# The first weights of an encoder trunk: a weight piece in two halves on two queues, a reordered load, and a store on another queue

## The chip, the cores and the metric

One core of a Trainium2 chip runs the whole program. The metric is the device time of one execution in microseconds (us); a comparison takes the median of several. In this program TensorE (PE) multiplies, VectorE (DVE), ScalarE (ACT) and GpSimd (POOL) work on its results, and SyncE (SP) starts most transfers. Each engine carries out its own instructions in order.

## The reference

Two sequences, a prompt of 2048 tokens and a sample of 512, with 1024 channels, pass through two layers and a final RMSNorm, all in float32:

```python
def attention_layer(x, g, w_in, w_out, sink, rel_bias):
    h = rmsnorm(x, g)
    z = h @ w_in
    q, k, v, gate = ...          # 1024, 256, 256 and 1024 columns; 16 heads, 4 kv heads
    o = banded_gqa_with_sink(q, k, v, rel_bias, sink)   # |i-j| <= 128
    return x + (o * jax.nn.silu(gate)) @ w_out

def fourier_layer(x, g, w_gate, w_out):
    h = rmsnorm(x, g)
    f = jnp.fft.fftn(hg, axes=(1, 3), norm="ortho").real   # 4 channel groups
    return x + (f * jax.nn.silu(h @ w_gate)) @ w_out
```

`rel_bias` gives each head a bias by the distance of query and key.

## The kernel before, in words

Every float32 product is made of three faster ones. An operand `a` is kept as a rounded part and a remainder (`hi`, `lo`), and `matmul3` (lines 90 to 94) issues hi by hi (L92), hi by lo (L93) and lo by hi (L94) into one PSUM bank. So each weight, once loaded in float32 (a tile `w32...`), is rounded by ACT (L113) and subtracted by DVE (L120) or POOL (L118) before PE can use it. `load_w` does this; a piece is 128 rows by 1024 columns, 512 KB. Pieces 8 and 9 of `w_in` hold the K weights, four blocks of 256 columns each: piece 8 has the blocks of k = 0 to 3 (k counts the eight blocks of 128 input channels), piece 9 those of k = 4 to 7. Pieces 10 and 11 hold the V weights in the same way. Pieces 0 to 7 are Q, 12 to 19 the gate.

The tokens go in chunks of 512. The sample is chunk 0 and comes first. For it `make_h(0, None)` loads the eight tiles `xk` of the transposed input (256 KB each, L180) and scales them by the norm's weight `g0s` into the two parts of `h` (ACT L186, DVE L187). The division by the root mean square comes later: `stats` loads the tokens a second time (`xs`, L149), squares and sums them on ACT (L150), and `inv_rms` makes the reciprocal root, ending in one POOL instruction (L87, `inv`). `spread` brings it into the layout of the products with four transposes on PE (L164).

At the very start PE runs 12 warm-up products on a zero tile (`idle`, L206). Then `kv_proj` makes K (`kp`, 48 products, k outermost), one small product `bp` for the bias rows (L222), and V (`vp`, 96 products of half the width, k outermost in four banks); its evictions are L317 and L318, K's L266 and L267. After that come Q and gate (`qp`, `gp`) of the first pair of heads, p = 0, and from then on attention for p in between Q and gate for p + 1.

`bias_rows` copies `bp` into the tile `brow` (DVE L224) and stores it in `rowd` in HBM (L225); each pair of heads reads its biases back from there (`b`, L381).

Which instruction stands where in an engine's order is decided when the program is built, by a scheduler with estimated costs; `after(...)` adds an order by hand. A transfer is started by an instruction in the order of one engine, its queue: SP for loads, POOL for the stores of the split weights (`wsd`, L122). A transfer's instruction that waits holds up all that stands behind it in that engine's order. The order on SP's queue at the start is: `g0s`, piece 8, eight `xk`, pieces 9 and 10, the one-hot table and the small tables for the bias, four `xs`, piece 11, the store of `rowd`, then Q and gate weights and the first `b`.

Of the kernel before, what the change touches and what calls it, by code (L numbers as in the profile page):

```python
# [9 lines left out]
F32R = mybir.dt.float32r  # L10
# [3 lines left out]
ALU = mybir.AluOpType  # L14
# [4 lines left out]
P = 128  # L19
D = 1024  # L20
# [11 lines left out]
LINE = 512  # L32
# [7 lines left out]
def f32(ap):  # L40
    return ap.bitcast(F32)
# [3 lines left out]
def encoder(  # L45
# [3 lines left out]
    PE, ACT, DVE, POOL, SP = nc.tensor, nc.scalar, nc.vector, nc.gpsimd, nc.sync  # L49
# [5 lines left out]
    wp = wstack.enter_context(tc.tile_pool(name="wp", bufs=1, side="right"))  # L55
# [5 lines left out]
    mhalf = cpool.tile([P, 8], F32, name="mhalf")  # L61
    POOL.memset(mhalf, -0.5)
    g0s = cpool.tile([P, KD], F32, name="g0s")
    SP.dma_start(g0s, g0.rearrange("(k p) -> p k", p=P))

    x1d = dram.tile([T, D], F32, name="x1d")
    s2d = [dram.tile([n, D], F32, name=f"s2d{i}") for i, n in enumerate((SEQ, DEC))]
# [7 lines left out]
    def bank(name):  # L75
        return psum.tile([P, 512], F32, tag="bank", name=name)

    def xtile(shape, dtype, name):
        return xp.tile(shape, dtype, align_bytes=LINE, tag="x", bufs=4, name=name)
# [16 lines left out]
    def load_w(c, n, name, lo_engine=None, late=None):  # L96

        w = wp.tile([P, 2, D], F32R, align_bytes=LINE, tag="w", bufs=4, name=f"w{name}")
        if c == 1 and n in AGAIN:
            w32 = xtile([P, D], F32, f"w32{name}")  # L100
            SP.dma_start(w32, w_in[n])
            ACT.copy(w[:, 0], w32)
            DVE.tensor_tensor(w[:, 1], w32, f32(w[:, 0]), ALU.subtract)
            POOL.dma_start(f32(wsd[n]), f32(w))
            return w[:, 0], w[:, 1]
        if c:
            SP.dma_start(f32(w), f32(wsd[n]))
            return w[:, 0], w[:, 1]
        w32 = stage[late is not None or n > 19 or n in (6, 7, 18, 19)](f"w32{name}")
        load = SP.dma_start(w32, w_in[n] if n < 20 else w_out[(n - 20) // 4, (n - 20) % 4])  # L110
        if late:
            after(load, late)
        ACT.copy(w[:, 0], w32)  # L113
        if lo_engine is None:

            for i in range(4):
                cs = slice(i * 256, i * 256 + 256)
                POOL.tensor_tensor(w[:, 1, cs], w32[:, cs], f32(w[:, 0, cs]), ALU.subtract)  # L118
        else:
            lo_engine.tensor_tensor(w[:, 1], w32, f32(w[:, 0]), ALU.subtract)  # L120
        if late or n not in LATE + AGAIN:
            (SP if lo_engine else POOL).dma_start(f32(wsd[n]), f32(w))  # L122
        return w[:, 0], w[:, 1]

    stage, res_tile, ready = [], [], {}

    def after(ins, anchor):

        if anchor is not None:
            tc.add_manual_dep(ins.ins, anchor.ins.name, ISSUE, reason="issue order")  # L130

    def attention_phase():

        with ExitStack() as es:
# [20 lines left out]
            def spread(c, inv, place=None):  # L155

                tok, lo_t, hi_t = CHUNKS[c]
                nt = min(640, hi_t - tok) // P
                invb = ap.tile([P, 640], F32, tag="invb", name=f"invb{c}")
                for i0 in range(0, nt, 4):  # L160
                    m = min(4, nt - i0)
                    ps = bank(f"ib{c}_{i0}") if place is None else place
                    for i in range(m):
                        PE.transpose(ps[:, i * P : (i + 1) * P], inv[:, i0 + i : i0 + i + 1].to_broadcast([P, P]), ident)  # L164
                    ACT.copy(invb[:, i0 * P : (i0 + m) * P], ps[:, : m * P])  # L165
                return invb

            def make_h(c, invb):

                tok, lo_t, hi_t = CHUNKS[c]  # L170
                n = min(640, hi_t - tok)
                hs, halo = [], []
                for k in range(KD):
                    if invb is None:
                        if k % 2 == 0:
                            xk2 = wp.tile([P, 2, CH], F32, align_bytes=LINE, tag="uT", bufs=8, name=f"xk{c}_{k}")
                        xk = xk2[:, k % 2]
                    else:
                        xk = xtile([P, D], F32, f"xk{c}_{k}")[:, :640]
                    SP.dma_start(xk[:, :n], xT[k * P : (k + 1) * P, tok : tok + n])  # L180
                    if invb is not None:
                        last_mul[0] = POOL.tensor_tensor(xk[:, :n], xk[:, :n], invb[:, :n], ALU.mult)
                        after(last_mul[0], last_evac[0])
                    h = main.tile([P, 2, CH], F32R, align_bytes=LINE, tag="hT", bufs=8, name=f"h{c}_{k}")
                    gk = g0s[:, k : k + 1]
                    hi = ACT.activation(h[:, 0, :], xk[:, :CH], AF.Copy, scale=gk)  # L186
                    lo = DVE.scalar_tensor_tensor(h[:, 1, :], xk[:, :CH], gk, f32(h[:, 0, :]), ALU.mult, ALU.subtract)  # L187
                    after(hi, last_u[0])
                    after(lo, last_u[1])
                    hs.append((h[:, 0], h[:, 1]))  # L190
                    if n > CH:
                        if k % 4 == 0:
                            hl = ap.tile([P, 4, 2, P], F32R, align_bytes=LINE, tag="qab", bufs=2, name=f"hl{c}_{k}")
                        ACT.activation(hl[:, k % 4, 0], xk[:, CH:], AF.Copy, scale=gk)
                        DVE.scalar_tensor_tensor(
                            hl[:, k % 4, 1], xk[:, CH:], gk, f32(hl[:, k % 4, 0]), ALU.mult, ALU.subtract
                        )
                        halo.append((hl[:, k % 4, 0], hl[:, k % 4, 1]))
                return hs, halo
# [6 lines left out]
                PE.matmul(ps, idle[:, :P], idle, start=True, stop=True)  # L206

            last_u = [None, None]
            early = [load_w(0, 8, "k0_0", DVE)]
            hs, halo = make_h(0, None)  # L210
            early.append(load_w(0, 9, "k0_1", DVE))

            def bias_rows():

                rowd = dram.tile([NH, 512], F32, name="rowd")
                rb = ap.tile([33, NH], F32, tag="tmp", bufs=2, name="rb")
                DVE.memset(rb[32:33], 1.0)
                SP.dma_start(rb[:32], rel_bias)
                oh = ap.tile([33, 512], F32, tag="s", bufs=2, name="oh")
                SP.dma_start(oh, onehot)  # L220
                bp = bank("bp")
                PE.matmul(bp[:NH], rb, oh, start=True, stop=True)  # L222
                brow = ap.tile([NH, 512], F32, tag="tmp", bufs=2, name="brow")
                DVE.tensor_copy(brow, bp[:NH])  # L224
                SP.dma_start(rowd, brow)  # L225
                sk = ap.tile([P, NH], F32, tag="sk", name="sk")
                SP.dma_start(sk, bass.AP(sink.tensor, sink.offset, [[0, P], [1, NH]]))
                DVE.tensor_scalar(sk, sk, -1.0, None, ALU.mult)
                return rowd, sk
# [390 lines left out]
            def first_norms():  # L620
                bias.extend(bias_rows())
                return [s() for s in stats(0)][-1]

            for c in range(len(CHUNKS)):

                if c > 1:
                    hs, halo = make_h(c, invb)
                for s in tail:
                    s()
                if c == 1:  # L630
                    hs, halo = make_h(c, invb)
# [4 lines left out]
                rowd, sk = bias  # L636
# [7 lines left out]
                for i in range(64 + LAG + AVLAG):  # L644
                    p, n = divmod(i, 8)
# [14 lines left out]
                    if c + 1 < len(CHUNKS):  # L660
# [4 lines left out]
                        elif i == 56:  # L665
                            invb = spread(c + 1, inv)
# [8 lines left out]
                    k = i - LAG  # L675
# [20 lines left out]
    def fourier_phase(tail):  # L696
        with ExitStack() as es:
# [522 lines left out]
            for i, f in enumerate(pend):  # L1220
                finish(*f, last=i == len(pend) - 1)

    fourier_phase(attention_phase())


# [96 lines left out]
```

## Time and profile before

| | us |
|---|---|
| three runs | 1663.11, 1664.0, 1667.96 |
| median | 1664.0 |
| the profiled execution | 1665.56 |
| its span, first to last instruction | 1663.8 |
| PE busy in it | 1640.0 |
| ACT busy in it | 873.8 |
| DVE busy in it | 1172.5 |

How to read the lines of a profile here: in the timeline, a row has its start and duration in us, the engine (PEld is PE's weight load, SPq the transfers that SP issues), the line of the kernel, the operation, the tile written and the tiles read with the shapes, how many instructions the row merges, and in brackets the idle time before it with what ended it. In the waits, a row names who waited for whom, with the total in us, the number of times and the longest.

### The profile page before, as it was taken

How to read it: one execution, taken by the hardware profiler on the slowest of the kernel's cores; microseconds unless marked ns; L12 is line 12 of the kernel's file. 1: busy time of each engine (PE TensorE's matmuls, PEld its weight loads, DVE VectorE, ACT ScalarE, POOL GpSimd, SP SyncE). 2: the span in 40 equal slices, each digit the busy share in tenths (PEclk: the TensorE clock that was granted, in tenths of full speed). 3: DMA queues.
4: the chain of work that ended last, by engine and by line, in shares of the span. 5: the costliest groups of instructions: out<-in, count | busy, mean ns of one | idle time of the engine just before them, and what ended most of it. 6: DMA issues, size and time to landing. Idle time of an engine off the chain costs nothing.

```text
span 1663.8 us, 25654 instructions
## 1 busy us (share of the span) xinstructions
PE 1640.0 (99%) x8987; PEld 1410.4 (85%) x8987; DVE 1172.5 (70%) x2810; ACT 873.8 (53%) x1998; POOL 382.3 (23%) x536
## 2 busy tenths in 40 slices
PE   9999999999999999999999999999999999999997
PEld 7888788888898888988888888888888887888886
DVE  5787665888548886478874688768676769888553
ACT  6788644676236674256752466555554545342321
POOL 2465642112402113121122211221111111101000
PEclk9999999999999999999999999999999999999999
DMA  7486886454864456754549644556556578553331
GB/s 276 162 303 232 286 329 227 160 194 156 289 227 164 159 190 221 249 206 155 189 146 329 231 158 158 225 197 230 184 199 234 184 247 319 165 190 125 113 127 51
DMA packets 90252, 340.49 MB, mean 205 GB/s; under 512 B 11099, under 2 KB 21339, under 8 KB 72716
## 3 DMA queue, kind: packets, MB, share of 16 engines
q1 hardware_dynamic: 71676, 261.50, 46.0%
q0 software_dynamic: 18160, 76.56, 11.8%
q8 instruction: 72, 1.18, 0.3%
q10 hardware_dynamic: 288, 0.79, 0.1%
q14 instruction: 56, 0.46, 0.1%
HBM read 263.28 MB, written 75.53 MB: 204 GB/s over the span
## 4 chain that ended last, share of the span: by engine, by line
PE 82%; DVE 5%; ACT 5%; DMA 4%; issue 2%; POOL 1%; SPq 0%; DVEq 0%; POOLq 0%; ACTq 0%
PE spt L404 5%; PE av L457 5%; PE pt L443 5%; PE qp L92 4%; PE qp L94 4%; PE qp L93 4%; PE gp L92 4%; PE gp L94 4%; PE gp L93 4%; PE op L92 4%; PE op L94 3%; PE op L93 3%; PE fo L93 3%; PE fo L94 3%; PE fo L92 3%
## 5 line engine op out<-in xcount | busy, mean ns | idle before, releaser
L420 ACT ACTIVATE S<-S 128x385 f32<-128x385 f32 (+1 forms) x320 | 191.0, 597 | 46.8 <-DVE S L416 45.3
L444 ACT CAST pts<-pt 128x384 fp32r<-128x384 f32 (+1 forms) x320 | 144.2, 453 | 109.1 <-PE pt L443 104.5
L445 DVE TENSOR_TENSOR pts<-pt,pts 128x384 fp32r<-128x384 f32 (+1 forms) x320 | 168.3, 527 | 43.9 <-ACT pts L444 40.7
L416 DVE CUSTOM_DVE_ANT_0 S<-spt,b 128x385 f32<-128x385 f32 (+1 forms) x320 | 168.8, 528 | 34.7 <-PE spt L404 31.6
L404 PE MATMUL spt<-kwin,qab 128*128 128x384 f32 (+1 forms) x640 | 157.2, 327 | 1.1 <-DVE S L416 1.1
L476 POOL TENSOR_TENSOR o<-o,s 128x256 f32<-128x256 f32 x75 | 55.4, 739 | 437.7 <-DVE o L474 437.4
L443 PE MATMUL pt<-ident,S 128*128 128x128 f32 x896 | 150.6, 273 | 0.7 <-ACT S L429 0.6
L404 PEld LDWEIGHTS spt<-kwin,qab 128*128 128x128 f32 x640 | 118.2, 188 | 26.9 <-DVE S L416 1.7
L457 PEld LDWEIGHTS av<-pts,v 128*128 128x128 f32 x896 | 126.4, 189 | 14.0 <-DVE qab L353 1.6
L92 PE MATMUL gp<-h,wg 128*128 128x512 f32 x320 | 137.8, 431 | 0.0
L92 PE MATMUL qp<-h,wq 128*128 128x512 f32 x320 | 136.9, 428 | 0.8 <-DVE v L318 0.8
L457 PE MATMUL av<-pts,v 128*128 128x256 f32 x896 | 136.1, 285 | 1.4 <-DVE qab L353 1.1
L92 PE MATMUL op<-wo,uT 128*128 128x512 f32 x320 | 126.5, 397 | 1.5 <-ACT invb L165 0.8
L92 PE MATMUL fo<-wo,tTu 128*128 128x512 f32 x320 | 125.8, 393 | 1.3 <-ACT wo L1124 1.3
L443 PEld LDWEIGHTS pt<-ident,S 128*128 128x128 f32 x896 | 113.6, 140 | 15.7 <-DVE pts L445 3.2
L94 PE MATMUL qp<-h,wq 128*128 128x512 f32 x320 | 126.1, 394 | 0.0
L94 PE MATMUL gp<-h,wg 128*128 128x512 f32 x320 | 125.9, 393 | 0.0
L93 PE MATMUL op<-wo,uT 128*128 128x512 f32 x320 | 125.8, 393 | 0.0
L93 PE MATMUL qp<-h,wq 128*128 128x512 f32 x320 | 125.8, 393 | 0.0
L93 PE MATMUL gp<-h,wg 128*128 128x512 f32 x320 | 125.7, 393 | 0.0
L93 PE MATMUL fo<-wo,tTu 128*128 128x512 f32 x320 | 125.4, 392 | 0.1
L94 PE MATMUL fo<-wo,tTu 128*128 128x512 f32 x320 | 124.7, 390 | 0.0
(356 smaller groups left out, 4089.6 us busy)
## 6 DMA issues: line engine op xcount, KB each, us to landing
wo<-wsd SPq DMA_DIRECT2D x32, 1024.0 KB, 5.0
wq<-wsd SPq DMA_DIRECT2D x31, 1024.0 KB, 4.9
wg<-wsd SPq DMA_DIRECT2D x31, 1024.0 KB, 6.4
x<-x1d SPq DMA_DIRECT2D x40, 512.0 KB, 3.9
b<-b21d SPq DMA_DIRECT2D x40, 512.0 KB, 5.8
b<-rowd SPq DMA_DIRECT2D x40, 384.0 KB, 4.4
xs<-in_x_dram SPq DMA_DIRECT2D x23, 512.0 KB, 6.8
s2d<-gt POOLq DMA_DIRECT2D x40, 256.0 KB, 3.7
```

The lines of the kernel that those rows point to most:

```text
L92: PE.matmul(out, a[0], b[0], start=start, stop=False, skip_group_check=more)
L93: PE.matmul(out, a[0], b[1], start=False, stop=False, skip_group_check=more)
L94: PE.matmul(out, a[1], b[0], start=False, stop=stop, skip_group_check=more)
L404: PE.matmul(ps[:, 2 + k0 * P : 2 + k1 * P], q, kwin[g][:, part, b * P + k0 * P : b * P + k1 * P], start=part == 0, stop=part == 1,)
L416: DVE.tensor_tensor_reduce(out=s[:, e0:e1], in0=ps[:, 1 + e0 : 1 + e1], in1=st["bias"][:, j, 386 - e1 : 386 - e0][:, ::-1], scale=1.0, sca ...
L420: last_exp[0] = ACT.activation(s[:, e0:e1], s[:, e0:e1], AF.Exp, bias=mn, scale=-1.0, accum_out=den)
L443: PE.transpose(ps[:, kb, :], s[:, 1 + kb * P : 1 + (kb + 1) * P], ident)
L444: ACT.copy(hi[:, k0:k1, j, :], ps[:, k0:k1, :])
L445: DVE.tensor_tensor(lo[:, k0:k1, j, :], ps[:, k0:k1, :], f32(hi[:, k0:k1, j, :]), ALU.subtract)
L457: PE.matmul(out, v, pt[:, kb].rearrange("p h q -> p (h q)"), start=kb == k0 and part == 0, stop=kb == k1 - 1 and part == 1,)
L476: eng.tensor_tensor(o, o, s, ALU.mult)
```

## The change

The first K weight piece (piece 8) is loaded as two halves of 512 columns, one by SP's queue and one by ACT's, and each half is rounded and subtracted by itself; the second half's two instructions stand behind `h` of k = 0. `g0s` is loaded by ACT's queue instead of SP's. Piece 9 is loaded, rounded and subtracted after `h` of k = 3 instead of after k = 7. The rows of the bias are stored by POOL's queue instead of SP's.

In the built program, on ACT the two transfers stand ahead of its table load. On PE, K's products at k = 1 and k = 4 change places among themselves, and in V at k = 4 the four rounded products and the four transposes of `spread` come before the first product that takes the remainder of piece 11. On ACT and DVE the rounding and subtracting of the first gate weights moves behind `spread`'s copy, and K's first evictions move a few places ahead. From the second pair of heads on, the instruction orders are the same.

```diff
     g0s = cpool.tile([P, KD], F32, name="g0s")
-    SP.dma_start(g0s, g0.rearrange("(k p) -> p k", p=P))
+    ACT.dma_start(g0s, g0.rearrange("(k p) -> p k", p=P))
...
-            def make_h(c, invb):
+            def make_h(c, invb, between={}):
...
                     hs.append((h[:, 0], h[:, 1]))
+                    if k in between:
+                        between[k]()
...
             last_u = [None, None]
-            early = [load_w(0, 8, "k0_0", DVE)]
-            hs, halo = make_h(0, None)
-            early.append(load_w(0, 9, "k0_1", DVE))
+
+            wk = wp.tile([P, 2, D], F32R, align_bytes=LINE, tag="w", bufs=4, name="wk0_0")
+            wk32 = stage[0]("w32k0_0")
+
+            def half(i):
+                cs = slice(i * 512, i * 512 + 512)
+                (SP, ACT)[i].dma_start(wk32[:, cs], w_in[8, :, cs])
+                return lambda: (
+                    tc.keep_in_program_order(ACT.copy(wk[:, 0, cs], wk32[:, cs])),
+                    DVE.tensor_tensor(wk[:, 1, cs], wk32[:, cs], f32(wk[:, 0, cs]), ALU.subtract),
+                )
+
+            halves = [half(i) for i in range(2)]
+            halves[0]()
+            early = [(wk[:, 0], wk[:, 1])]
+            hs, halo = make_h(0, None, {0: halves[1], 3: lambda: early.append(load_w(0, 9, "k0_1", DVE))})
...
                 DVE.tensor_copy(brow, bp[:NH])
-                SP.dma_start(rowd, brow)
+
+                POOL.dma_start(rowd, brow)
```

## The prediction

> **What bounds the kernel now.** I read the page's busy shares first, then PE's waits, then the timeline of the first 35 us, because every line of the change acts before that.
>
> ```profile
> PE 1640.0 (99%) x8987; PEld 1410.4 (85%) x8987; DVE 1172.5 (70%) x2810; ACT 873.8 (53%) x1998; POOL 382.3 (23%) x536
> PE kp L92 <- ACT h L186: 2.0, 1, 2.0
> PE qp L92 <- DVE v L318: 0.8, 1, 0.8
> SPq L225 <- DVE inv L86: 8.0, 1, 8.0
> ```
>
> PE is busy for 1640.0 of 1663.8 us, so 23.8 us of idle time is all that any reordering can win. The second line, from PE's waits, is the longest single one: 2.0 us before the first K product. The third is the gap before the first Q product. The last, from SP's queue, is the store of the bias rows, which holds SP for 8.0 us. All three lie where the change acts. The profiled execution took 1665.56 us (span 1663.8 and 1.76 around it), 1.56 above the median of 1664.0.
>
> The start, by the timeline:
>
> ```profile
> 1.18 4.07 PE L206 MATMUL idle<-idle 128*128 128x512 bf16 x12 [1.18 <-DVE idle L203]
> 0.73 0.44 SPq L64 DMA_DIRECT2D g0s<-in_g_dram  x1
> 1.23 0.57 SPq L110 DMA_DIRECT2D w32k<-in_w_in_dram  x1
> 5.58 1.04 ACT L113 CAST wk<-w32k 128x1024 fp32r<-128x1024 f32 x1 [3.57 <-DMA w32k<-in_w_in_dram]
> 6.53 5.01 ACT L186 ACTIVATE h<-xk,g0s 128x512 fp32r<-128x512 f32 x8
> 6.65 1.23 DVE L120 TENSOR_TENSOR wk<-w32k,wk 128x1024 fp32r<-128x1024 f32 x1 [4.29 <-ACT wk L113]
> 7.30 1.22 PE L92 MATMUL kp<-h,wk 128*128 128x512 f32 x2 [2.04 <-ACT h L186]
> 7.80 5.38 DVE L187 SCALAR_TENSOR_TENSOR h<-xk,g0s,h 128x512 fp32r<-128x512 f32 x8
> 8.60 0.79 PE L93 MATMUL kp<-h,wk 128*128 128x512 f32 x1
> 19.91 0.39 PE L94 MATMUL kp<-h,wk 128*128 128x512 f32 x1
> ```
>
> The warm-up ends at 5.25. The first weight piece (512 KB, issued at 1.23 behind g0s) lands at 5.58. ACT rounds it, then makes h of k=0; DVE takes the weight's low part (6.65 to 7.88) and only then h's (7.80 on), so the third K product starts at 8.60. The last of the 48 starts at 19.91; one step is 5.01/8 = 0.63 us on ACT and 5.38/8 = 0.67 on DVE.
>
> The granted clock and the transfers, from the windows (duration, PE, PEld, DVE, ACT, POOL, clock, DMA share, GB/s):
>
> ```profile
> 2.00:2.50 0.50, 0.50 (x3) 0.21 (x2) 0.33 (x2) 0.01 (x1) 0.00 (x0) 1.00 0.67 5
> 2.50:3.00 0.50, 0.50 (x3) 0.22 (x2) 0.00 (x0) 0.00 (x0) 0.00 (x0) 1.00 2.18 133
> 3.00:3.50 0.50, 0.50 (x3) 0.17 (x2) 0.00 (x0) 0.00 (x0) 0.00 (x0) 1.00 0.06 25
> 7.00:7.50 0.50, 0.20 (x1) 0.20 (x2) 0.50 (x1) 0.50 (x2) 0.00 (x0) 0.79 1.03 393
> 7.50:8.00 0.50, 0.50 (x2) 0.30 (x2) 0.50 (x2) 0.50 (x2) 0.00 (x0) 0.50 1.03 389
> 10.50:11.00 0.50, 0.50 (x3) 0.46 (x2) 0.50 (x2) 0.50 (x2) 0.00 (x0) 0.80 0.99 410
> 5.00:10.00 5.00, 2.88 (x7) 1.66 (x6) 3.35 (x5) 4.42 (x7) 0.00 (x0) 0.73 1.06 404
> ```
>
> A mean of 0.79 between 1.00 and 0.50 puts the fall at 7.29, one of 0.80 the recovery at 10.70: 3.41 us apart. In the 3.41 us before the fall (from 3.88) PE worked only 5.25 - 3.88 = 1.37 us, 40%. So the gap before the first K product costs twice: 2.0 us of waiting, then 3.4 us at half clock. Meanwhile the transfer engines are occupied but move almost nothing until 3.5 (5, 133, 25 GB/s): g0s's 1024 four-byte pieces go first. After that they run at 404 GB/s.
>
> **The change, part by part.** *First half of the weight piece.* It is the first transfer on SP, issued at 0.73 instead of 1.23, and half as big. The old one took 5.58 - 1.23 = 4.35 us, of which 1.30 is 512 KB at 404 GB/s; 3.05 is latency and g0s. Kept whole, that gives 0.73 + 3.05 + 0.65 = 4.43; with g0s's slow 1.0 us out of its way 3.4. I take 4.0. ACT now issues g0s and the second half itself, ahead of its table load: at the SP rows' 0.44 and 0.57 that ends near 1.75, hidden under the wait for data. The x tile of k=0 follows on SP while the second half shares the engines: 0.65 to 1.3 us more, 4.1 to 5.7; I take 4.9. ACT rounds half a piece in 0.53 (half of 1.04), h starts at 4.9, and the first K product at about 5.6 instead of 7.30. DVE subtracts half a piece in 0.62, and is free when h is rounded: third product at 6.4 (5.5 to 7.1) instead of 8.60. That is 2.2 us.
>
> *The clock.* In the same 3.41 us PE would now work 1.37 us of warm-up and about 1.3 of products, 2.7 or 79%. I take it that the clock stays full. Then 46 products from 6.4 at (19.91 - 10.81)/40 = 0.23 us each end at 16.9.
>
> ```profile
> 10.81 0.40 PE L93 MATMUL kp<-h,wk 128*128 128x512 f32 x1
> 12.05 1.05 ACT L113 CAST wk<-w32k 128x1024 fp32r<-128x1024 f32 x1 [0.51 <-DMA w32k<-in_w_in_dram]
> 13.14 1.23 DVE L120 TENSOR_TENSOR wk<-w32k,wk 128x1024 fp32r<-128x1024 f32 x1
> ```
>
> [...]
>
> *Second weight piece ahead of x tiles 4 to 7.* It lands after 2.1 MB instead of after 3.1: 5.2 us at 404 GB/s from about 2.9, and some 0.9 until it is seen, 9.0 instead of 12.05. Its cost is that it now stands ahead of h 4 to 7 on ACT (1.05) and DVE (1.23): rounded at 10.1, low part at 11.3, h of k=4 complete at 12.0. PE wants that at 6.4 + 23 x 0.23 = 11.7, so it waits 0.3. K ends at about 17.3 instead of 19.91 + 0.23 = 20.14: **2.8 us**, the first term. From best to worst times of data, 1.0 to 3.7.
>
> *V projection.* Its second weight piece becomes the limit:
>
> ```profile
> 13.62 0.33 SPq L110 DMA_DIRECT2D w32v<-in_w_in_dram  x1
> 20.40 1.06 ACT L150 ACTIVATE xs<-xs 128x1024 f32<-128x1024 f32 x1
> 21.64 1.05 ACT L113 CAST wv<-w32v 128x1024 fp32r<-128x1024 f32 x1
> 23.41 1.22 DVE L120 TENSOR_TENSOR wv<-w32v,wv 128x1024 fp32r<-128x1024 f32 x1
> 27.04 0.40 PE L92 MATMUL vp<-wv,h 128*128 128x256 f32 x2
> ```
>
> It is rounded after the four squares of xs, which the full-rate transfers pace, so I leave its 24.63 where it was. PE would need it from 27.04 - 2.8 = 24.24, and the changed order puts four high products and four transposes (about 0.8 us) in front of the first product that needs the low part. So 2.8 passes; much more than 3.2 would not, unless the transfers begin earlier too.
>
> *Bias rows on POOL's queue.* They pass POOL's only early instruction:
>
> ```profile
> 21.29 0.68 DVE L224 COPY brow<-bp 16x512 f32<-16x512 f32 x1 [5.00 <-PE bp L222]
> 22.00 0.33 SPq L225 DMA_DIRECT2D rowd<-brow  x1
> 22.20 1.04 POOL L87 TENSOR_TENSOR inv<-inv,mhalf 128x4 f32<-128x4 f32 x1 [20.90 <-DVE inv L86]
> 22.43 0.37 SPq L110 DMA_DIRECT2D w32q<-in_w_in_dram  x1
> 36.47 0.78 POOL L122 DMA_DIRECT2D wsd<-wq  x1 [0.32 <-DVE kwin L267]
> 32.20 1.05 ACT L113 CAST wq<-w32q 128x1024 fp32r<-128x1024 f32 x1 [2.50 <-DMA w32q<-in_w_in_dram]
> 33.16 0.83 ACT L317 ACTIVATE v<-vp,vsc 128x256 fp32r<-128x256 f32 x2
> 34.19 0.50 PE L92 MATMUL qp<-h,wq 128*128 128x512 f32 x1 [0.82 <-DVE v L318]
> ```
>
> A POOL issue costs up to 0.78. With K earlier it is over before the reciprocal root (L87); otherwise it delays that by some 0.6, for which spread and the V scales have slack until 27. SP no longer stands still: the first Q and gate weights follow the second V weights (13.62) at about 14 instead of 22.43, and the piece of p=1 follows the bias load. That ends the last gap: V's first eviction (33.16) stood on ACT behind the rounding of p=1's Q weights (32.20), which waited for their transfer. With those down by about 28, the 0.82 us before 34.19 shrinks to about 0.1: **0.7 us**, the second term (0 to 0.8). If the eviction stays behind a late transfer, it is nothing.
>
> From the first Q product on, instruction order is the same in both programs, apart from K's evictions at the same place, and PE is the busy engine, so I let the whole shift reach the end. Sum: 2.8 + 0.7 = 3.5 us; 1665.56 becomes 1662.1, and against the median **1660.5**.
>
> **The rivals.** *The clock falls all the same* (chance 0.17): if products begin near 7 or the phase is bad, 3.41 us at half clock lose half of that, 1.7 us. Left: 1.8, 1662.2. The 40% window shows that 40% is too little; nothing shows whether 79% is enough.
>
> *g0s comes late* (0.22; the one on the other side). Alone in front, its pieces took about a microsecond. Now they share the engines with large pieces.
>
> ```profile
> DMA packets 1902, 1.85 MB, mean 231 GB/s; under 512 B 1130, under 2 KB 1130, under 8 KB 1902
> ```
>
> In the first 8 us 1130 packets are small and 772 large, 2.4 KB on average. If each small one waits for a large one, g0s's 1024 wait for 2.4 MB, 6 us: it lands near 8.5, every h needs it, and the second half stands behind it on ACT's queue. [...]
>
> *The shift is absorbed later* (0.08): 1664.0.
>
> ```profile
> 60.00:200.00 140.00, 135.98 (x772) 116.50 (x771) 107.85 (x369) 115.52 (x284) 83.24 (x120) 1.00 0.71 253
> ```
>
> For it, PE is idle for 4.0 of the 140 us after 60, so something other than PE sets some of the pace; against it, what it waits for there starts from earlier work, which moves with it.
>
> **How the numbers follow.** The forecast has 0.53. About 0.3%, 5 us, is what a measurement of this kernel can tell from no change: below 1659.0 is faster. The forecast's upper end is 3.7 + 0.8 = 4.5, and an earlier start of all transfers (up to 1 us) carries it past 5: with the spread of the runs (1663.11 to 1667.96) a good half of it falls there or on the border. I give faster 0.35, same 0.50. Slower has 0.15: the late g0s at its far end. The range reaches from 1656.0 (5 us, and 3 for the spread) to 1667.0 (the late g0s and its neighbours). The forecast's own is 1658.5 to 1663.
>
> **What would show it.** Right: first K product before 6, clock 1.00 from 7 to 11, last K product before 17.5, SP's Q-weight load near 14, no gap before the first Q product. Wrong: h of k=0 waiting for g0s, half clock past 7.3, or PE waiting in V for its second weight piece.

## The result, and the profile after

| | before | after |
|---|---|---|
| median, us | 1665.66 (22 runs, 1662.86 to 1669.69) | 1663.3 (22 runs, 1661.6 to 1668.2) |
| the profiled execution | 1665.56, span 1663.8 | 1665.08, span 1663.3 |

The ratio of after to before is 0.9987, with a 95% interval of 0.9981 to 0.9993. That is 2.2 us saved, between 1.2 and 3.2, and within the 0.3% that the prediction called no change. The two profiled executions differ by less, 0.5 us, and why they do is the main question of what follows.

The start, by the timeline of the changed kernel:

```profile
1.18 5.07 PE L208 MATMUL idle<-idle 128*128 128x512 bf16 x12 [1.18 <-DVE idle L205]
4.19 0.62 ACT L219 CAST wk<-w32k 128x512 fp32r<-128x512 f32 x1 [1.06 <-DMA w32k<-in_w_in_dram]
5.50 0.72 ACT L186 ACTIVATE h<-xk,g0s 128x512 fp32r<-128x512 f32 x1 [0.69 <-DMA xk<-in_xT_dram]
6.27 0.73 PE L92 MATMUL kp<-h,wk 128*128 128x512 f32 x2
7.06 0.50 PE L93 MATMUL kp<-h,wk 128*128 128x512 f32 x1
9.27 1.05 ACT L113 CAST wk<-w32k 128x1024 fp32r<-128x1024 f32 x1 [0.53 <-DMA w32k<-in_w_in_dram]
17.42 0.39 PE L94 MATMUL kp<-h,wk 128*128 128x512 f32 x1
13.91 0.36 SPq L110 DMA_DIRECT2D w32q<-in_w_in_dram  x1
19.80 0.71 POOL L241 DMA_DIRECT2D rowd<-brow  x1 [18.49 <-DVE brow L239]
23.61 0.38 SPq L397 DMA_DIRECT2D b<-rowd  x1
29.29 1.05 ACT L113 CAST wq<-w32q 128x1024 fp32r<-128x1024 f32 x1 [0.62 <-DMA w32q<-in_w_in_dram]
31.28 0.50 PE L92 MATMUL qp<-h,wq 128*128 128x512 f32 x1 [0.39 <-DVE v L334]
```

The first half lands by 4.19, the first K product starts at 6.27 instead of 7.30, the last at 17.42 instead of 19.91, and the first Q product at 31.28 instead of 34.19. So 2.91 us are gained by then. The Q weights are loaded at 13.91 instead of 22.43. The windows after (duration, then PE, PEld, DVE, ACT, POOL, clock, DMA share, GB/s) show the clock at 1.00, where it stood at 0.50 from 7.29 to 10.70 before:

```profile
3.50:7.00 3.50, 3.48 (x9) 1.05 (x7) 1.44 (x3) 2.10 (x4) 0.00 (x0) 1.00 0.97 324
7.00:10.50 3.50, 3.44 (x16) 2.87 (x16) 2.74 (x6) 2.97 (x5) 0.00 (x0) 1.00 1.05 412
```

Next, SP's loads of the biases, and ACT's squaring of the next chunk's tokens, `xs`, from the timeline. First the kernel before, and last its row of PE's waits from 130 to 185 us (total, times, longest):

```profile
134.65 0.38 SPq L381 DMA_DIRECT2D b<-rowd  x1
135.12 1.52 SPq L149 DMA_DIRECT2D xs<-in_x_dram  x2
136.06 0.58 POOL L122 DMA_DIRECT2D wsd<-wq  x1 [0.30 <-POOL wq L118]
141.22 1.06 ACT L150 ACTIVATE xs<-xs 128x1024 f32<-128x1024 f32 x1 [2.22 <-DMA xs<-in_x_dram]
156.61 0.38 SPq L381 DMA_DIRECT2D b<-rowd  x1
PE pt L443 <- ACT S L429: 0.6, 2, 0.3
```

Then the changed kernel, in the same order:

```profile
131.70 0.38 SPq L397 DMA_DIRECT2D b<-rowd  x1
132.17 2.00 SPq L149 DMA_DIRECT2D xs<-in_x_dram  x2
133.09 0.59 POOL L122 DMA_DIRECT2D wsd<-wq  x1 [0.30 <-POOL wq L118]
140.55 1.06 ACT L150 ACTIVATE xs<-xs 128x1024 f32<-128x1024 f32 x1 [4.50 <-DMA xs<-in_x_dram]
155.94 0.38 SPq L397 DMA_DIRECT2D b<-rowd  x1
PE pt L459 <- ACT S L445: 2.8, 2, 2.5
```

At 131.70 the lead is still 2.95. At 155.94 it is 0.67. In between ACT waits 4.50 us for its fourth token tile (2.22 before), the softmax `S` queued behind it on ACT comes late, and PE waits 2.8 us for that (0.6 before). The load was issued at 132.17, and 0.92 us later POOL stores 1 MB of split Q weights (piece 6, `wsd<-wq`) beside it: from 133.09 to the square at 140.55 the transfer engines' share is 1.00 to 1.02. Before, the store follows 0.94 us behind the load (135.12, 136.06), so the pair itself has moved as one. Farther on, like products of PE show a lead of 0.6 to 0.8 until 1100 us, a lag of 0.6 from 1180 to 1380, and a lead of 0.5 at the end: single executions also drift by more than 1 us far from the change.

### The profile page after: what moved, and what is told of

It is laid out like the page before. It is cut to its first block, busy times and chain, and to the rows that moved or that the text cites. A ratio compares the mean times of both kernels' runs of the same rounds, so it can differ in the third digit from the quotient of the medians.

```text
span 1663.3 us, 25657 instructions
## 1 busy us (share of the span) xinstructions
PE 1641.2 (99%) x8987; PEld 1411.0 (85%) x8987; DVE 1171.7 (70%) x2811; ACT 874.1 (53%) x1999; POOL 383.3 (23%) x537
## 3 DMA queue, kind: packets, MB, share of 16 engines
q10 hardware_dynamic: 1472, 1.05, 0.2%
## 4 chain that ended last, share of the span: by engine, by line
PE 81%; DVE 5%; ACT 5%; DMA 4%; issue 3%; POOL 2%; SPq 0%; POOLq 0%; DVEq 0%; ACTq 0%
PE spt L420 5%; PE av L473 5%; PE pt L459 5%; PE qp L92 4%; PE qp L94 4%; PE qp L93 4%; PE gp L92 4%; PE gp L94 4%; PE gp L93 4%; PE fo L93 4%; PE fo L94 4%; PE op L92 4%; PE fo L92 4%; PE op L94 3%; PE op L93 3%
```

## The experiments

All kernels, with the start of K's last product, of the first Q product, ACT's wait for the fourth `xs` tile, and the span, each from its one profiled execution (us), and the ratio to the kernel before:

| kernel | K last | Q first | wait for xs | span | ratio, 95% |
|---|---|---|---|---|---|
| before | 19.91 | 34.19 | 2.22 | 1663.8 | |
| after | 17.42 | 31.28 | 4.50 | 1663.3 | 0.9987 (0.9981 to 0.9993) |
| a1: before, store moved | 19.02 | 32.82 | 2.94 | 1661.4 | 0.9999 (0.9990 to 1.0008) |
| a2: after, store back on SP | 17.44 | 32.96 | 4.38 | 1665.9 | 0.9992 (0.9983 to 1.0002) |
| a3: after, piece 9 back | 18.66 | 32.74 | 4.16 | 1663.9 | 1.0003 (0.9993 to 1.0012) |
| b4: after, piece 8 whole | 18.09 | 32.60 | 4.73 | 1663.6 | 0.9989 (0.9979 to 0.9999) |
| b2: after, `g0s` on SP | 17.64 | 31.19 | 1.88 | 1660.5 | 0.9986 (0.9975 to 0.9997) |
| a4: after, `xs` earlier | 17.42 | 31.74 | none | 1660.8 | 0.9985 (0.9976 to 0.9994) |
| b1: before, `xs` earlier | 20.50 | 33.98 | none | 1663.3 | 0.9996 (0.9987 to 1.0005) |
| a5: after, two stores left out | 17.97 | 31.60 | 1.16 | 1658.9 | 0.9966 (0.9954 to 0.9978) |
| b3: before, longer warm-up | 18.86 | 33.61 | 2.00 | 1661.9 | 0.9999 (0.9988 to 1.0010) |
| c1: after, two stores held | 17.53 | 31.38 | 0.93 | 1657.7 | 0.9967 (0.9954 to 0.9981) |
| c2: before, two stores held | 20.48 | 34.78 | 1.49 | 1660.7 | 0.9983 (0.9974 to 0.9992) |
| c3: after, once more | 18.22 | 31.70 | 3.40 | 1662.5 | one run, 1664.31 |

### a1: the store alone

The kernel before, with one line changed.

```diff
-                SP.dma_start(rowd, brow)
+                POOL.dma_start(rowd, brow)
```

> The kernel before with one part of the change: the bias rows stored by POOL's queue. Theory A (the gap before the first Q product comes from late Q weights behind the store on SP): the first Q and gate weights are issued near 14 instead of 22.43 us, the first Q product starts near 33.7 instead of 34.19, and the whole is 0.3 to 0.6 us shorter, hardly to be told from none. Theory B (the store's move is most of the gain): the whole is shorter by 1.5 to 2.5 us. Theory C (the store on POOL is slower and its reader late): the load that follows the first bias load is issued after 25.5 instead of at 24.94 and the gap stays at 0.8; no gain.

The gap before the first Q product fell from 0.82 to 0.33, about what it is in the changed kernel. K's last product came at 19.02, though nothing ahead of it is changed: in this execution the clock did not fall. Without that, some 0.5 us is left at the first Q product, close to theory A. The ratio, 0.9999, shows no gain; 0.5 us lie inside its interval.

```profile
32.82 0.50 PE L92 MATMUL qp<-h,wq 128*128 128x512 f32 x1 [0.33 <-DVE v L318]
```

### a2: the start alone

The changed kernel, with that line put back.

```diff
-                POOL.dma_start(rowd, brow)
+                SP.dma_start(rowd, brow)
```

> The changed kernel with the bias rows stored by SP's queue again, as before; the two halves, g0s on ACT's queue and the second piece's place stay. Theory A: first Q product at 31.3 to 31.8 us (31.28 in the changed kernel), the whole within 0.5 us of the changed one, 1.7 to 2.4 below the kernel before. Theory B (the store's move is most of the gain): within 0.7 us of the kernel before, first Q product after 33.

K is as in the changed kernel, 17.44, but the first Q product is 1.68 later, which theory A (31.3 to 31.8) did not foresee. The timeline says why: in this build the store stands ahead of the load of V's second weight piece on SP's queue and holds it up until 19.91 (first two rows; in the changed kernel that load goes out at 13.46). So PE waits in V for the rounded piece and then for its remainder (last two rows).

```profile
19.54 0.33 SPq L241 DMA_DIRECT2D rowd<-brow  x1
19.91 0.42 SPq L110 DMA_DIRECT2D w32v<-in_w_in_dram  x1
25.77 0.74 PE L92 MATMUL vp<-wv,h 128*128 128x256 f32 x4 [0.60 <-ACT wv L113]
27.03 0.39 PE L93 MATMUL vp<-wv,h 128*128 128x256 f32 x1 [0.52 <-DVE wv L120]
```

So in these executions, with the earlier K, the store's queue is worth 1.68 by the first Q product, against 0.5 with the old K. The two parts are not independent.

### a3: piece 9 again behind all x tiles

```diff
-            hs, halo = make_h(0, None, {0: halves[1], 3: lambda: early.append(load_w(0, 9, "k0_1", DVE))})
+            hs, halo = make_h(0, None, {0: halves[1]})
+            early.append(load_w(0, 9, "k0_1", DVE))
```

> The changed kernel with the second K weight piece loaded and split after the last x tile, as before; halves, g0s and store stay as changed. Theory A (the reorder is what lets K run through): the piece is seen near 12 us, PE waits for its remainder at k = 4 until about 14.2, the last K product starts near 19 instead of 17.42, the first Q product near 32.9, and 1.4 to 1.8 us of the gain are gone at that place. Rival (K would run through without it, the x tiles bound it anyway): last K product within 0.5 us of 17.42.

PE waits 0.60 in the middle of K for the rounded piece, and K's last product is at 18.66, 1.24 later than in the changed kernel; the first Q product is 1.46 later. The time is that of the kernel before. The order of piece 9 is the largest part.

```profile
12.94 0.50 PE L92 MATMUL kp<-h,wk 128*128 128x512 f32 x1 [0.60 <-ACT wk L113]
```

### b4: piece 8 whole again

```diff
...
-            halves = [half(i) for i in range(2)]
-            halves[0]()
-            early = [(wk[:, 0], wk[:, 1])]
-            hs, halo = make_h(0, None, {0: halves[1], 3: lambda: early.append(load_w(0, 9, "k0_1", DVE))})
+            early = [load_w(0, 8, "k0_0", DVE)]
+            hs, halo = make_h(0, None, {3: lambda: early.append(load_w(0, 9, "k0_1", DVE))})
```

> The changed kernel with the first K weight piece whole, first on SP's queue, rounded and subtracted in one; g0s on ACT's queue, the second piece's place and the store stay as changed. Theory (half a piece saves 0.4 us of rounding and 0.5 of subtracting ahead of h, and 256 KB ahead of the first x tile): first K product at 6.8 to 7.1 instead of 6.27, third at 8.0 to 8.3 instead of 7.06, last K product near 18.4, first Q product near 32.2. Rival (the start is bound by the x tile, the halves hide nothing): third product within 0.3 us of 7.06.

The first K product is at 6.66, 0.39 later than with halves, the third at 7.75 (7.06), and K ends 0.67 later. By the first Q product it is 1.32, because the gap there is 1.05 in this execution instead of 0.39. K's times lie 0.1 to 0.6 ahead of what was expected, the first Q product 0.4 behind. The ratio is that of the changed kernel within the intervals.

```profile
6.66 0.73 PE L92 MATMUL kp<-h,wk 128*128 128x512 f32 x2 [0.75 <-ACT h L186]
7.75 0.50 PE L93 MATMUL kp<-h,wk 128*128 128x512 f32 x1 [0.36 <-DVE h L187]
32.60 0.50 PE L92 MATMUL qp<-h,wq 128*128 128x512 f32 x1 [1.05 <-DVE v L321]
```

### b2: `g0s` in front of SP's queue again

```diff
-    ACT.dma_start(g0s, g0.rearrange("(k p) -> p k", p=P))
+    SP.dma_start(g0s, g0.rearrange("(k p) -> p k", p=P))
```

> The changed kernel with g0s first on SP's queue again, ahead of the first half; the second half stays on ACT's. Theory (g0s's small pieces cost what follows them on the same queue about a microsecond): first half seen near 5.0 instead of 4.2 us, first K product near 6.9 instead of 6.27, first Q product near 31.9. Rival (beside the second half on the other queue g0s is just as dear): within 0.3 us of the changed kernel at the first K product.

The first half is seen at 4.71 instead of 4.19, `h` of k = 0 starts at 5.75 instead of 5.50, and still waits for the x tile. The first K product is at 6.52, 0.25 later, which is the rival's range. K ends 0.22 later, Q starts 0.09 earlier. So this part of the change is worth nothing that these runs can tell.

```profile
4.71 0.62 ACT L219 CAST wk<-w32k 128x512 fp32r<-128x512 f32 x1 [2.22 <-DMA w32k<-in_w_in_dram]
5.75 0.72 ACT L186 ACTIVATE h<-xk,g0s 128x512 fp32r<-128x512 f32 x1 [0.42 <-DMA xk<-in_xT_dram]
```

### a4 and b1: the fourth `xs` tile earlier, in the kernels after and before

Both have the same edit: in the sample's attention, the fourth step of `stats` (load and square) stands at step 38 instead of 40.

```diff
-                        if i >= 28 and i % 4 == 0 and norm_steps:
+                        if i in ((28, 32, 36, 38, 44, 48) if c == 0 else range(28, 64, 4)) and norm_steps:
```

> The changed kernel with one other thing changed: in the first chunk, the load and square of the fourth token tile for the next chunk's norm stand ahead of the loads for the sixth pair of heads, not behind its bias load. Theory P (the start's 2.9 us are lost again at 140 us, where ACT waits 4.5 us for that load, which shares the engines with a POOL store): that wait goes, the shift against the kernel before stays at 2.9 or more after 157 us, and the whole is 4 to 6 us below the kernel before. Rival Q (another wait near 140 to 180 takes its place, since ACT is nearly full there): the shift is again under 1 us after 157, the whole 0.5 to 2.5 us below the kernel before.

> The kernel before, with the fourth token tile's load and square for the next chunk's norm ahead of the loads for the sixth pair of heads, as in the run a4. It tells whether the wait at 140 us is the change's own or the kernel's. Theory P (the wait is the kernel's own, between 2 and 4.5 us by chance): 1 to 2.5 us below the kernel before. Rival (only the changed start makes that load late): within 0.8 us of the kernel before. [...]

ACT's wait for the tile is gone in both, and with it PE's waits for `S` behind it (2.8 us in the changed kernel, 0.6 in the kernel before). PE's waits from 100 to 185 us show one new one, in the two kernels alike: 0.9 us for rounded Q weights. The other long one, for a softmax step (1.3, and 1.1 in b1), is no replacement: the kernels before and after have it too, at 1.1. The rows of a4:

```profile
PE spt L420 <- DVE S L432: 1.3, 1, 1.3
PE qp L92 <- ACT wq L113: 0.9, 1, 0.9
```

The waits listed there come to 5.8 us in the changed kernel and 3.5 in a4, to 3.6 in the kernel before and 3.3 in b1. But the ratios are those of the kernels that they were made from, so no gain on average can be told, and the 4 to 6 us of theory P did not come. With the wait gone in both, the profiled spans differ by 2.5 us, and the ratios by 0.11%.

### a5: without the stores of pieces 6 and 18

```diff
-            SP.dma_start(f32(w), f32(wsd[n]))
+            SP.dma_start(f32(w), f32(wsd[n - 1 if n in (6, 18) else n]))
...
-        if late or n not in LATE + AGAIN:
+        if late or n not in LATE + AGAIN + (6, 18):
```

> The changed kernel without the two stores of split weights that POOL starts near 133 and 137 us (pieces 6 and 18); the later chunks read the pieces before them instead, so they compute with other weights. Theory P (the fourth token tile's load comes late at 140 us because it shares the engines with those stores): the load is seen within 5 us of its issue instead of 8.4, ACT's wait for it falls from 4.5 to below 1.5 us, the shift against the kernel before after 157 us is 2.9 or more, and the whole is 3 to 6 us shorter than the kernel before. Rival R (the load is late because of the bias load ahead of it on its own queue): the wait stays above 3 us and the shift after 157 is again below 1.

The wait is 1.16, the span 1658.9, and the ratio 0.9966: some 5 us below the kernel before, where the changed kernel is 2.2 below it. As 2 MB of transfers are gone as well, this run can't tell whether the stores' place or their bytes cost that; c1 can.

```profile
137.21 1.06 ACT L150 ACTIVATE xs<-xs 128x1024 f32<-128x1024 f32 x1 [1.16 <-DMA xs<-in_x_dram]
```

### b3: a longer warm-up before the old start

```diff
-WARM = 12
+WARM = 16
```

> The kernel before the change with 16 warm-up products instead of 12, which end near 6.1 to 7.0 us and still before the first K product at 7.3. If the clock's fall is what makes K long at the old start (theory C), K's last product starts between 18.6 and 19.2 us, as in the kernel with only the store moved (19.02, where the clock did not fall), not at 19.9 or 20.5, and the granted clock stays at 1.00 from 5 to 14 us; the time falls by 0 to 0.9 us. [...]

PE goes from the warm-up into K without a gap, the clock stays at 1.00, and K's last product is at 18.86 instead of 19.91, as expected, although the warm-up ran until 7.70. Half of that is lost at the first Q product, where the gap is 1.28 instead of 0.82, and no gain in the time can be measured.

```profile
3.50:7.00 3.50, 3.50 (x9) 1.21 (x8) 0.73 (x1) 1.74 (x3) 0.00 (x0) 1.00 0.98 337
7.00:10.50 3.50, 3.45 (x15) 2.41 (x14) 3.50 (x6) 3.50 (x6) 0.00 (x0) 1.00 1.06 408
```

### c1 and c2: the two stores held back, in the kernels after and before

Nothing is left out; the same edit in both puts the two stores some steps later in POOL's order, behind the tokens' loads. They are issued 6.0 and 11.8 us later than in the changed kernel (c1), 6.9 and 12.7 later than in the kernel before (c2); some 10 and 5 were expected.

```diff
-        if late or n not in LATE + AGAIN:
+        if n in (6, 18):
+            held.append((n, w))
+        elif late or n not in LATE + AGAIN:
...
+                    if c == 0 and i in (44, 44 + 2):
+                        n6, w6 = held.pop(0)
+                        after(POOL.dma_start(f32(wsd[n6]), f32(w6)), last_exp[0])
```

> The changed kernel, with POOL's stores of the split Q piece 6 and gate piece 18 issued some 10 and 5 us later on POOL's queue (nothing left out). Theory S (the wait of ACT for the load of xs_3 near 140 us is paid because POOL's store of the q piece shares the transfer engines with that load): the wait falls from 4.50 us in the changed kernel to at most 1.5, SP's b load of the last pair of the sample issues between 152.0 and 153.8 instead of at 155.94, and the ratio is near 0.997 (1660 to 1661.5 us). Rival (the stores only move the crowding to the next loads, of the tokens, weights or biases near 150 us): b load at 155 or later, or a new wait of over 1.5 us between 140 and 185, and the ratio stays at 0.9987 or above.

> The kernel before the change, with the same two stores held back. If the start's shift is real and is only eaten by the wait near 140 us, this kernel's b load of the last pair lies 1.5 to 3.0 us later than that of the changed kernel with stores held back, and its time is 1.5 to 3.0 us longer than that one's, with a ratio to the kernel before between 0.997 and 0.9995. If the change's shift is absorbed in any case (something else than PE sets the pace there), the two kernels with held stores are within 0.7 us of each other.

The medians are 1659.5 (c1) and 1662.36 (c2), 2.86 apart. In c1 the wait is 0.93, and PE's waits for `S` behind it come to 0.6 instead of 2.8. The timeline of c1, with the store now behind the square, and last that row of PE's waits:

```profile
131.61 0.38 SPq L399 DMA_DIRECT2D b<-rowd  x1
132.08 1.97 SPq L151 DMA_DIRECT2D xs<-in_x_dram  x2
136.90 1.06 ACT L152 ACTIVATE xs<-xs 128x1024 f32<-128x1024 f32 x1 [0.93 <-DMA xs<-in_x_dram]
139.10 0.59 POOL L691 DMA_DIRECT2D wsd<-wq  x1
150.35 0.38 SPq L399 DMA_DIRECT2D b<-rowd  x1
PE pt L461 <- ACT S L447: 0.6, 2, 0.3
```

The timeline of c2:

```profile
134.93 0.38 SPq L383 DMA_DIRECT2D b<-rowd  x1
140.76 1.06 ACT L152 ACTIVATE xs<-xs 128x1024 f32<-128x1024 f32 x1 [1.49 <-DMA xs<-in_x_dram]
154.19 0.38 SPq L383 DMA_DIRECT2D b<-rowd  x1
```

The first Q products are 3.40 apart, the bias loads 3.32 and 3.84, and the spans 3.0: of the lead at the start, which here includes a fall of c2's clock, all but 0.3 to 0.4 us reaches the end when the stores are out of the way. The last bias load of c1 is earlier than expected (150.35 against 152.0 to 153.8), and 3.84 from c2's, more than the 1.5 to 3.0 expected: c2's clock fell at 8.67 (7.29 in the kernel before), and its last K product started at 20.48. c1 is faster than both kernels: 0.33% below the one before, 0.46 to 0.19 by the interval.

In c2, PE's waits for `S` behind the tile are 0.6, as in the kernel before, so c2's own gain (0.17%) was not made there. It starts 0.59 later than the kernel before at the first Q product and is 1.65 ahead at the first product of the output projection `op` (176.39 against 178.04). In between, the wait of 1.1 for the softmax step is gone, and the last one, ahead of `op`, is 0.3 instead of 0.8. What in the held stores removes these was not tested.

### c3: the changed kernel once more

> The changed kernel, unaltered, once more. If the wait at xs_3 is a matter of how the packets fall, it differs from 4.50 us by more than 0.5 in this execution, and the b load of the last pair moves with it from 155.94, while K's last product stays within 0.2 of 17.42 and the first Q product within 0.5 of 31.28. If the wait follows from the order of instructions alone, it is 4.5 within 0.3.

The wait was 3.40 instead of 4.50, so it varies from one execution to the next by more than 1 us, and the last bias load moved with it, from 155.94 to 154.78. K missed what was expected: its last product was at 18.22, 0.80 later, because the first x tile was seen at 6.32 instead of 5.50. At the first Q product, at 31.70 with no gap ahead of it, 0.42 of that is left.

```profile
6.32 0.72 ACT L186 ACTIVATE h<-xk,g0s 128x512 fp32r<-128x512 f32 x1 [1.45 <-DMA xk<-in_xT_dram]
```

## Why the prediction was right, point by point

**The number.** 1660.5 was predicted and 1663.3 measured, inside the range, and no change within 0.3%, the likeliest of the three cases. Of the 2.8 between them, 1.66 is the kernel before, whose median was 1665.66 in this comparison and not 1664.0. The rest is the gain: 3.5 predicted, 2.36 measured by the medians, 2.2 by the ratio. So the time lies just above the forecast's own range of 1658.5 to 1663.

**First K product: predicted 0.67 too early.** The first half came at 4.19 as thought (4.0). The x tile behind it was put at 4.9, and was seen at 5.50 and 6.32 in the two executions; ACT's row names it as what `h` waited for. The third product was 7.06 instead of 6.4. A second bound was overlooked: the warm-up itself ran until 6.25 here, and would have held a product at 5.6.

**The clock: right.** In all nine profiled executions of the changed kernel and its variants it stayed at 1.00 (so in every row from 3.50 to 12.08 of b4, c1 and c3). In those with the old start and the short warm-up it fell in three of four (before at 7.29, b1 at 8.47, c2 at 8.67; not in a1). The prediction counted the fall as belonging to the kernel before, and a1 shows the price: where the clock did not fall, the old K's last product started at 19.02. The runs show these moments and not what sets them; the rival's bad phase was not shown. Products at half clock count as busy (from 8.67 to 12.08 c2 has 3.41 us of PE busy with 9 products at 0.50, c1 3.41 with 17 at 1.00), so the 23.8 us of idle time were not all that a reordering could win, as the prediction's first paragraph has it.

**K: right to 0.3.** The first term was 2.8 and is 2.49 (19.91 to 17.42). It is the sum of a late start (0.67 too late) and a better middle: piece 9 was rounded at 9.27 and PE never waited for it. Against a1, at full clock on both sides, it is 1.60; the rest, 0.89, is clock. The parts by themselves: 1.24 for the order of piece 9 (a3), 0.67 for the halves (b4), 0.22 for `g0s` (b2). Each is from one execution. The unaltered kernel's K ended 0.80 later in c3, so the last two lie within what one execution differs from another; the first has PE's wait and the time of a3 beside it.

**V's second piece: no limit, as predicted,** but for another reason than the one given. It was not left at 24.63: the last square of `xs` started at 18.63 instead of 20.40, and DVE subtracted the piece from 21.76 for 1.22 us, so it was ready at 22.98. PE first took the remainder at 25.38. With the store on SP (a2) it is a limit. That the store's queue would also decide this was missed.

**The gap before Q: 0.43 of 0.7 in the profiled pair, and not shown on average.** It shrank from 0.82 to 0.39. The Q weights of p = 0 went out at 13.91, as predicted (14). But those of p = 1 stand behind the first bias load on SP's queue, and that waits for `rowd`: the store is issued by POOL at 19.80 and lands 3.8 us later (1.6 from SP's queue in the kernel before), so the bias load goes out only at 23.61. So the piece is rounded at 29.29, not by 28, and V's first eviction still stands behind it. The gap varies: it was zero in c3 and b2 and 0.84 in a4, and zero with the store on SP too, in b1. The store was not over before the reciprocal root either, which stood behind it on POOL and started at 20.53, some 0.5 late; PE did not wait for it.

```profile
rowd<-brow POOLq DMA_DIRECT2D x1, 32.0 KB, 3.8
```

**"I let the whole shift reach the end": the step that failed in the profiled pair, but not shown to fail on average.** There the lead falls from 2.95 to 0.67 between 131.70 and 155.94, at the wait for `xs`. This was the rival to which the prediction gave 0.08, and the argument against it, that what PE waits for there moves with PE, was true of the load's issue and not of its landing. What it costs PE follows ACT's wait. The nine executions with the stores in their place, by ACT's wait for the tile, and PE's waits for `S` behind it (us):

| | b2 | b3 | before | a1 | c3 | a3 | a2 | after | b4 |
|---|---|---|---|---|---|---|---|---|---|
| ACT for `xs` | 1.88 | 2.00 | 2.22 | 2.94 | 3.40 | 4.16 | 4.38 | 4.50 | 4.73 |
| PE for `S` | 0.3 | 0.3 | 0.6 | 1.3 | 1.8 | 2.2 | 2.7 | 2.8 | 2.8 |

A wait of 2 us costs PE next to nothing, and each further one about 0.9. c1 and c2 show that the shift arrives without the stores beside the load. It also arrived in b2 with the stores in place, where the wait was short: 3.00 at the first Q product (34.19 to 31.19), 3.3 in the span (1663.8 to 1660.5).

"All is absorbed" is not what the medians say. The change is worth 0.13% with the stores in place, 0.16% with them held (c1 against c2) and 0.11% with the tile loaded earlier (a4 against b1), and the intervals overlap. So a loss on average is not shown, and the profiled pair shows a bad draw. The larger part of what is missing from 3.5 was missing at the start: the first Q product was 2.91 earlier in the profiled pair, and 2.78 on average between the five executions with the new start unaltered (after, a4, a5, c1, c3: 31.54) and the three with the old one (before, b1, c2: 34.32). The measured 2.2, 1.2 to 3.2 by its interval, agrees with a shift of 2.78 that reaches the end.

**What stays open.** The wait is larger with the new start: 1.88 to 4.73 in six executions with the stores in their place (mean 3.84), 2.00 to 2.94 in three with the old one (mean 2.39). The load and the store beside it are issued at the same distance, 0.92 or 0.94 us, in the two profiled kernels. Whether the difference is chance or made by something that runs beside them was not settled.

**The other rivals.** `g0s` late: from the issues of transfers in the first 9 us (KB each, us from issue to landing), after and then before:

```profile
g0s<-in_g_dram ACTq DMA_DIRECT2D x1, 4.0 KB, 4.0
```

```profile
g0s<-in_g_dram SPq DMA_DIRECT2D x1, 4.0 KB, 2.4
```

It took 4.0 us instead of 2.4. It now goes at the same time as large pieces and by another queue; which of the two costs the 1.6 was not tested. It is far from what this rival reckoned with, a landing near 8.5 after 6 us of waiting for large pieces. It came before the x tile, and b2 shows nothing to be had from it. That each small piece waits for a large one was the author's estimate, and 4.0 us contradict it; no run shows the late `g0s` that the upper end of the range and the chance of slower counted on. The clock falling all the same: not seen.

## What to carry to other kernels

In a single execution, a lead won at the start can be lost at the next wait for a transfer, so after a change at one end look for the place where the two traces' distance changes, not only at the place of the edit. Stores that nobody needs soon should not be issued just behind a load that an engine in the critical chain is about to wait for: here, holding two of them for 6 to 13 us (0.17% in c2) was worth about as much as the whole reordered start (0.13%), though in c2 by waits behind that load and not at it. One profiled execution has a draw in it, of the clock's fall (in three of the four with the old start and the short warm-up) and of the transfers (for `xs` the changed kernel waited 4.50 us in one and 3.40 in the other); a part's price should be taken from two kernels with the same draw, or from many runs.

## What the runs showed of the hardware

**How busy PE was ahead of the clock's fall.** The 3.41 us that end with the fall, as long as the clock then stood at 0.50, in the kernel before, b1 and c2:

```profile
3.88:7.29 3.41, 1.38 (x7) 0.39 (x4) 0.64 (x1) 1.71 (x3) 0.00 (x0) 1.00 1.03 396
```

```profile
5.06:8.47 3.41, 1.52 (x6) 0.47 (x4) 1.72 (x2) 2.80 (x4) 0.00 (x0) 1.00 1.05 395
```

```profile
5.26:8.67 3.41, 1.57 (x6) 0.55 (x5) 2.10 (x3) 2.90 (x4) 0.00 (x0) 1.00 1.04 386
8.67:12.08 3.41, 3.41 (x9) 2.65 (x10) 3.41 (x6) 3.31 (x5) 0.00 (x0) 0.50 1.04 416
```

PE was busy for 40, 45 and 46% of them. In a5, whose warm-up took 4.05 us against 4.07 in the kernel before, the same stretch as there was 54% busy, and the clock stayed:

```profile
3.86:7.27 3.41, 1.83 (x9) 0.70 (x7) 1.17 (x2) 1.82 (x3) 0.00 (x0) 1.00 0.99 358
```

Whether a border lies between 46 and 54%, and whether the busy share of just these stretches decides, was not shown. In programs with the same start the clock fell at 7.29, 8.47 and 8.67; it stood at 0.50 for 3.41 us in the kernel before (7.29 to 10.70) and in c2 (8.67 to 12.08).

**The granted clock does not show the warm-up.** The rows above give 1.00 for 3.50 to 7.00 in the changed kernel, while its twelve warm-up products took 5.07 us, against 4.07 in the kernel before. At first their weight loads start 0.43 us apart in both (2.01, 2.44, 2.87). In the changed kernel that lasts until the last one at 5.42; in the kernel before the last five lie within 1.04 us, the last two 0.21 apart (4.45, 4.66), with 1.00 granted there too (4.00 to 5.00). Only this spacing, 0.43 against 0.21, tells the two rates apart.

**A store on POOL's queue beside a load on SP's.** In the changed kernel the square of the fourth `xs` tile starts 8.4 us after SP's instruction for its load (132.17 to 140.55), with a 1 MB store of POOL issued 0.92 us behind it. In c1, without the store beside it, it is 4.8 us (132.08 to 136.90). The nine executions with that store in its place range from 5.8 to 8.6 us, the three without it (c1, c2, a5) from 4.8 to 5.4.
